# Second feed-forward of a decoder layer: 19 gate/up tiles as seven products of halves

## The chip, the cores and the metric

One core of a Trainium2 chip runs the whole layer in one launch. The metric is the device time of one execution in microseconds, lower is better. Everything is float32; the matmuls take float32r operands.

## The reference, cut to what matters

```python
for l in range(DEPTH):
    ...
    y = rmsnorm(h, ffn1_pre_g[l]) * (1.0 + sc1) + sh1
    y = swiglu(y, ffn1_w_gate[l], ffn1_w_up[l], ffn1_w_down[l])
    h = h + FFN_RESIDUAL_WEIGHT * g1 * rmsnorm(y, ffn1_post_g[l])
    ...
    y = rmsnorm(h, ffn2_pre_g[l]) * (1.0 + sc3) + sh3
    y = swiglu(y, ffn2_w_gate[l], ffn2_w_up[l], ffn2_w_down[l])
    h = h + FFN_RESIDUAL_WEIGHT * g3 * rmsnorm(y, ffn2_post_g[l])

def swiglu(y, w_gate, w_up, w_down):
    return (jax.nn.silu(y @ w_gate) * (y @ w_up)) @ w_down
```

512 tokens, width 1024, hidden width 2816. Between the two feed-forwards stands a token mixing by mLSTM and HGRN2 heads. The shift, scale and gate vectors come from a product of the conditioning c with `ada_w`.

## The kernel before, in words

Each float32 product is made of three matmuls (`mm3`, L110 to L113): an operand is split into a rounded part hi (a cast to float32r) and a rest lo (raw minus hi), and hi x hi, hi x lo and lo x hi are added up in PSUM. `unit` (L95) loads 128 x 1024 weights into one of four raw buffers (pool `wraw`) by SyncE's DMA queue, casts them to hi on ScalarE (L106) and subtracts to lo on VectorE (L107); hi and lo have four buffers each in the pool `wsp`.

The activations stay in SBUF transposed, width on the partitions: `y` is a pair of tiles of 8 k-tiles x 512 tokens. `y_token_tile` (L189) makes them for 128 tokens: TensorE transposes, scale and shift out of PSUM (four k-tiles on ScalarE, four on VectorE), rounding and rest.

The second feed-forward (`ffn2`, L798) has 22 tiles of 128 hidden units, each with a gate and an up part. Its first three tiles (`FF2_F`) run in two halves of 256 tokens, since tokens 256 to 511 come late: two `y_token_tile` calls are still in `later` and are issued between their matmuls. Four of their six weight units lie in `wsp`; those of the third tile lie in parts of `hT` that are not yet used. The other 19 tiles go through `up_tile` (L227): two units, two PSUM tiles, 2 x 8 x 3 matmuls of 512 columns, then `swiglu_evac` (L216): sigmoid on ScalarE, two products on VectorE, a cast on ScalarE and a subtract on VectorE, into the pair `hT`. After each of the first 11 of these tiles one step of `rest` is issued: eight `ada` (L118, a 512 KB load and four multiply-reduces on VectorE), `gate_rows`, nothing, and `gate_load`.

`down` (L236) multiplies `hT` with the down weights: two halves of 512 output columns, 11 units of two hidden tiles each, four token tiles of 128, in four PSUM tiles; the last four units run token tile by token tile, so that the normalisation (`post`, L284) of one goes beside the next.

The order on each engine is that of a list scheduler, which places instructions by their place in the program where nothing holds them back. A buffer is handed on when the last reader in the program is done. PSUM has six `mm` buffers and two `tr` buffers. `phase` reserves some bytes ahead of a pool, so that the tiles behind it lie at other addresses.

Of the kernel before, what the change touches and what calls it, by code (L numbers as in the profile page):

```python
# [7 lines left out]
F32 = mybir.dt.float32  # L8
F32R = mybir.dt.float32r
# [5 lines left out]
P = 128  # L15
# [6 lines left out]
NH = 4  # L22
EPS = 1e-6
START_F = 3
GAP_W = 160
GAP_Y = 64
GAP_H = 128
GAP_M = 64
FF2_F = 3

# [2 lines left out]
def layer_kernel(ctx: ExitStack, tc: tile.TileContext, x, c, cols, gate_b,  # L33
# [14 lines left out]
    def phase(pool, name, nbytes):  # L48

        if nbytes:  # L50
            pool.tile([P, nbytes // 4], F32, name=name)

    phase(gap, "gap_w", GAP_W)

# [55 lines left out]
    def mm3(ps, lhs, rhs, start, stop):  # L110
        nc.tensor.matmul(ps, lhs[0], rhs[0], start=start, stop=False)  # L111
        nc.tensor.matmul(ps, lhs[0], rhs[1], start=False, stop=False)  # L112
        nc.tensor.matmul(ps, lhs[1], rhs[0], start=False, stop=stop)  # L113
# [42 lines left out]
    def rstd_of(ss, n, w, name):  # L156
# [32 lines left out]
    def y_token_tile(s, i, y, n):  # L189

        ts_ = slice(i * P, (i + 1) * P)
        for q in range(2):
# [19 lines left out]
            nc.vector.tensor_tensor(out=y[1][:, q * 4:q * 4 + 4, ts_], in0=yf, in1=hv.bitcast(F32),  # L212
                                    op=ALU.subtract)


    def swiglu_evac(f, psg, psu, hT, tag):  # L216
# [16 lines left out]
                    k == 0, k == KT - 1)  # L233
        swiglu_evac(f, ps[0], ps[1], hT, tag)

    def down(wd, hT, tag, s, nxt, n=NF, order=lambda f: f, pump=None, drain=None, rest=()):  # L236


        t0, ss0, later = [], [], []
# [1 line left out]
        for half in range(2):  # L241
            acc = [mm_tile(f"pd{tag}_{half}_{i}") for i in range(NT)]

            def step(u, i, v):
                for e in range(2):
                    f = order(2 * u + e)
                    mm3(acc[i], (hT[0][:, f, i * P:(i + 1) * P], hT[1][:, f, i * P:(i + 1) * P]),
                        (v[0][:, e, :], v[1][:, e, :]), u == 0 and e == 0, u == nu - 1 and e == 1)

            last = []  # L250
            for u in range(nu):
                v = unit(wd[half, u], 1024, f"d{tag}_{half}_{u}")
                v = tuple(a.rearrange("p (e n) -> p e n", e=2) for a in v)
                if rest:
                    rest.pop(0)()
                if u < nu - 4 or (drain and half == 0):
                    if drain and u == nu - 1:
                        drain()
                    for i in range(NT):
                        step(u, i, v)  # L260
                        if pump:
                            pump()
                else:
                    last.append((u, v))
            for i in range(NT):
# [530 lines left out]


    def ffn2(y, later):  # L798
        with tc.tile_pool(name="hT2", bufs=1) as hp:
            phase(hp, "gap_h2", GAP_H)  # L800
            hT = (hp.tile([P, NF, T], F32R, name="hThi2"), hp.tile([P, NF, T], F32R, name="hTlo2"))
            us = []
            for f in range(FF2_F):
                us.append([])
                for g in range(2):
                    dst = None
                    if f == FF2_F - 1:
                        sl = slice(NF - 2 * (g + 1), NF - 2 * g)
                        dst = tuple(a[:, sl, :].rearrange("p a b -> p (a b)") for a in hT)
                    us[f].append(k3(unit(wgu2[f, g], 1024, f"b_{f}_{g}", dst)))  # L810
# [15 lines left out]
            for f in range(FF2_F, NF):  # L826
                up_tile(f, wgu2, y, hT, "b")
                if rest:
                    rest.pop(0)()
            down(wd2, hT, "b", 2, None)  # L830

    ffn2(*mix(*ffn1()))

# [74 lines left out]
```

## Time and profile before

| | us |
|---|---|
| median of 3 runs | 1054.83 (1054.58 to 1054.88) |
| the profiled execution | 1054.96 |
| its span, first to last instruction | 1053.2 |
| 19 tiles, first matmul to the down projection's first | 717.3 to 926.0 |
| down projection | 926.0 to 1046.9 |

Times in rows count from the span's start. PE is TensorE's matmul, PEld its weight load, DVE VectorE, ACT ScalarE, POOL GpSimd, SP SyncE. L111 is line 111 of the kernel. A row of a timeline has start, duration, engine, line, operation, what is written and read, shapes, and in brackets the idle time before it and what ended it. Matmuls are pipelined: their starts are closer together than they last.

### The profile page before, as it was taken

What the parts mean: (1) busy time and instruction counts of PE and PEld (TensorE: products, weight loads), DVE (VectorE), ACT (ScalarE), POOL (GpSimd) and SP (SyncE); (2) the same over time, 40 slices, a digit from 0 to 9 for tenths busy, and PEclk for the clock granted to TensorE, in tenths of its full rate; (3) what the DMA queues carried; (4) which work ended last, traced back from release to release, by engine and by line L of the source; (5) the groups of instructions that cost most, each with busy time, mean ns of one, the idle gap of its engine ahead of it and who ended that gap; (6) DMA issues with size and microseconds to landing.
All of it is one profiled execution on the core that took longest, in us unless ns stands there. A gap on an engine that the chain in (4) does not pass through costs nothing.

```text
span 1053.2 us, 13118 instructions
## 1 busy us (share of the span) xinstructions
PE 1031.8 (98%) x4988; PEld 857.2 (81%) x4988; DVE 600.4 (57%) x1426; ACT 344.8 (33%) x496; POOL 70.7 (7%) x104
## 2 busy tenths in 40 slices
PE   6999999999999999999999999999999999999997
PEld 4778888888888878978888887898888888888886
DVE  7975465566555285387879775775543433332323
ACT  5542233222212164435343223632322222221311
POOL 1000000000000020022223131100000000000000
PEclk9999999999999999999999999999999999999999
DMA  9864445555655413333223311144454223322212
GB/s 343 279 212 152 147 153 156 164 158 165 197 180 166 149 63 126 107 124 111 100 81 100 101 61 61 44 153 146 138 111 149 92 89 101 100 99 81 100 40 80
DMA packets 42938, 136.39 MB, mean 130 GB/s; under 512 B 7670, under 2 KB 8054, under 8 KB 42876
## 3 DMA queue, kind: packets, MB, share of 16 engines
q1 hardware_dynamic: 42588, 135.41, 39.7%
q8 instruction: 39, 0.64, 0.2%
q10 hardware_dynamic: 288, 0.16, 0.1%
q14 instruction: 23, 0.19, 0.1%
HBM read 133.43 MB, written 2.12 MB: 129 GB/s over the span
## 4 chain that ended last, share of the span: by engine, by line
PE 86%; DVE 8%; issue 1%; DMA 1%; POOL 1%; ACT 1%; DVEq 0%; POOLq 0%; SPq 0%; ACTq 0%
PE pub L111 7%; PE pub L113 7%; PE pub L112 7%; PE pua L112 7%; PE pua L111 7%; PE pua L113 7%; PE pft L113 4%; PE pft L112 4%; PE pft L111 4%; PE pdb L112 4%; PE pdb L111 4%; PE pdb L113 4%; PE pda L111 4%; PE pda L113 3%; PE pda L112 3%; PE pl L576 3%
## 5 line engine op out<-in xcount | busy, mean ns | idle before, releaser
L111 PE MATMUL pub<-yhi,h_b 128*128 128x512 f32 (+1 forms) x368 | 137.8, 375 | 0.0
L113 PE MATMUL pub<-yhi,l_b 128*128 128x512 f32 (+1 forms) x368 | 137.0, 372 | 0.0
L112 PE MATMUL pub<-ylo,h_b 128*128 128x512 f32 (+1 forms) x368 | 136.0, 370 | 0.0
L111 PE MATMUL pua<-yhi,h_a 128*128 128x512 f32 x304 | 119.3, 392 | 0.7 <-DVE ta L219 0.7
L112 PE MATMUL pua<-ylo,h_a 128*128 128x512 f32 x304 | 119.8, 394 | 0.0
L113 PE MATMUL pua<-yhi,l_a 128*128 128x512 f32 x304 | 118.0, 388 | 0.0
L106 ACT CAST h_b<-r_b 128x1024 fp32r<-128x1024 f32 x42 | 44.0, 1051 | 137.8 <-issue 102.3
L107 DVE TENSOR_TENSOR l_b<-r_b,h_b 128x1024 fp32r<-128x1024 f32 x42 | 51.3, 1224 | 60.3 <-ACT h_b L106 60.3
L132 DVE CUSTOM_DVE_ANT_0 a<-a,sc 128x256 f32<-128x256 f32 x216 | 82.4, 425 | 0.0
L113 PEld LDWEIGHTS pub<-yhi,l_b 128*128 128x128 f32 x368 | 69.1, 188 | 13.4
L111 PE MATMUL pft<-yhi,h_ft 128*128 128x512 f32 x192 | 79.6, 415 | 0.0
L112 PEld LDWEIGHTS pub<-ylo,h_b 128*128 128x128 f32 x368 | 69.1, 188 | 13.0 <-DVE ylo L212 0.2
L106 ACT CAST h_a<-r_a 128x1024 fp32r<-128x1024 f32 x38 | 39.9, 1049 | 119.5 <-issue 74.9
L111 PEld LDWEIGHTS pub<-yhi,h_b 128*128 128x128 f32 x368 | 69.1, 188 | 11.3
L113 PE MATMUL pft<-yhi,l_ft 128*128 128x512 f32 x192 | 76.3, 397 | 0.0
L112 PE MATMUL pft<-ylo,h_ft 128*128 128x512 f32 x192 | 75.8, 395 | 0.0
L111 PE MATMUL pda<-h_da,hThi 128*128 128x512 f32 x176 | 69.5, 395 | 0.0
L112 PE MATMUL pdb<-l_db,hThi 128*128 128x512 f32 x176 | 69.3, 394 | 0.0
L113 PE MATMUL pda<-h_da,hTlo 128*128 128x512 f32 x176 | 69.0, 392 | 0.0
L111 PE MATMUL pdb<-h_db,hThi 128*128 128x512 f32 x176 | 69.0, 392 | 0.0
L111 PEld LDWEIGHTS pua<-yhi,h_a 128*128 128x128 f32 x304 | 57.1, 188 | 14.5 <-DVE ta L219 1.2
L112 PE MATMUL pda<-l_da,hThi 128*128 128x512 f32 x176 | 68.3, 388 | 0.0
(270 smaller groups left out, 1946.5 us busy)
## 6 DMA issues: line engine op xcount, KB each, us to landing
a<-in_ada_w_dram SPq DMA_DIRECT2D x70, 512.0 KB, 3.8
r_b<-in_wgu_dram SPq DMA_DIRECT2D x44, 512.0 KB, 3.5
r_a<-in_wgu_dram SPq DMA_DIRECT2D x38, 512.0 KB, 4.1
r_ft<-in_w_ft_dram SPq DMA_DIRECT2D x24, 512.0 KB, 3.8
r_da<-in_wd_dram SPq DMA_DIRECT2D x22, 512.0 KB, 3.4
r_db<-in_wd_dram SPq DMA_DIRECT2D x22, 512.0 KB, 3.5
r_dm<-in_w_out_dram SPq DMA_DIRECT2D x8, 512.0 KB, 4.4
r_s<-in_wgu_dram SPq DMA_DIRECT2D x12, 256.0 KB, 6.1
```

Source lines behind the costliest of these rows:

```text
L106: nc.scalar.copy(hi, raw)
L107: nc.vector.tensor_tensor(out=lo, in0=raw, in1=hi.bitcast(F32), op=ALU.subtract)
L111: nc.tensor.matmul(ps, lhs[0], rhs[0], start=start, stop=False)
L112: nc.tensor.matmul(ps, lhs[0], rhs[1], start=False, stop=False)
L113: nc.tensor.matmul(ps, lhs[1], rhs[0], start=False, stop=stop)
L132: nc.vector.tensor_tensor_reduce(out=raw[:, sl], in0=raw[:, sl], in1=sc[:, sl], scale=1.0, scalar=init if q == 0 else 0.0, op0=ALU.mult, o ...
L576: nc.tensor.matmul(pv[:, i, :], kk[:, sl], qq[:, sl], start=True, stop=True)
```

## The change

The 19 tiles are computed by Winograd's form of Strassen's scheme: seven products of halves in place of eight. A tile's weights are four blocks of 512 x 128: B11 and B21 are the upper and lower half (in k) of the gate weights, B12 and B22 those of the up weights; the activations are split into A11, A12 (first 256 tokens, k-tiles 0 to 3 and 4 to 7), A21 and A22. Sums of the A blocks (S1 to S4) are made once, sums of the B blocks (T1 to T4) for every tile, each split into hi and lo. A product is 4 k-tiles x 3 matmuls of 256 columns. The results are added up partly in PSUM and partly on ScalarE and VectorE. `hT` becomes one float32 tile, split into hi and lo per down unit and half (`split`). The ada and gate steps go into `down`.

```diff
-GAP_W = 160
+GAP_S = 160
+GAP_W = 32
+GAP_X = 192
...
+    phase(small, "gap_s", GAP_S)
...
-    def down(wd, hT, tag, s, nxt, n=NF, order=lambda f: f, pump=None, drain=None, rest=()):
+    def down(wd, hT, tag, s, nxt, n=NF, order=lambda f: f, pump=None, drain=None, rest=(), split=None):
...
+                    if split:
+                        x = tuple(a[:, e, i * P:(i + 1) * P] for a in v[2])
...
+                if split:
+                    v = (*v, split(half, u))
+                for _ in range(2 if split and u < 3 else 1):
+                    if rest:
+                        rest.pop(0)()
...
     def ffn2(y, later):
...
+            def sums(i, yfs):
...
+                tt(out=r[:, 0], in0=yfs[0], in1=yfs[1], op=ALU.add)
+                tt(out=r3, in0=hi1, in1=yfs[0], op=ALU.subtract)
+
+                def rest_of():
+                    tt(out=r[:, 1], in0=r[:, 0], in1=hi1, op=ALU.subtract)
+                    nc.scalar.copy(Shi[:, 0, :, a], r[:, 0])
+                    tt(out=r[:, 1], in0=r[:, 1], in1=lo1, op=ALU.subtract)
+                    tt(out=r3, in0=r3, in1=lo1, op=ALU.add)
+                    nc.scalar.copy(Shi[:, 1, :, a], r[:, 1])
+                    nc.scalar.copy(Shi[:, 2, :, a], r3)
...
+                    tt(out=s4[:, :, a], in0=hi2, in1=r[:, 1], op=ALU.subtract)
+                    tt(out=s4[:, :, a], in0=s4[:, :, a], in1=lo2, op=ALU.add)
+
+                late.append(rest_of)
...
+            us = [[k3(unit(wgu2[f, g], 1024, f"b_{f}_{g}")) for g in range(2)] for f in range(FF2_F)]
...
-                                later.pop(0)()
+                                later.pop(0)(hook=sums)
...
-                        swiglu_evac(f, ps[f][0], ps[f][1], hT, "b")
+                        t = small.tile([P, T], F32, tag="x2", name=f"sg_{f}")
+                        nc.scalar.activation(t, ps[f][0], AF.Silu)
+                        tt(out=hT[:, f, :], in0=t, in1=ps[f][1], op=ALU.mult)
+                if hf == 0:
+                    for fn in late:
+                        fn()
...
+                def load(self):
+                    pool, tag = ((hp, "Rb"), (small, "G"))[(self.f - FF2_F) % 2]
+                    self.Rb = pool.tile([P, D], F32, tag=tag, name=f"Rb{self.f}", bufs=1)
+                    nc.sync.dma_start(self.Rb, wgu2[self.f, 1])
...
+                def split(self, hl, raw):
+                    for sl in (slice(0, T), slice(T, 2 * T)):
+                        nc.scalar.copy(hl[0][:, sl], raw[:, sl])
+                    tt(out=hl[1], in0=raw, in1=hl[0].bitcast(F32), op=ALU.subtract)
+
+                def prep1(self):
+                    self.split(self.pair("B11", "B21", wsp, ("hi", "lo"), "1"), self.Ra)
+                    h4, l4 = self.pair("B22", None, small, ("ysb", "ysb"), "4", bufs=4)
+                    nc.scalar.copy(h4, self.Rb[:, T:])
...
+                def prep2(self):
...
+                    tt(out=Rb[:, T:], in0=Rb[:, T:], in1=Rb[:, :T], op=ALU.subtract)
+                    tt(out=Rb[:, :T], in0=Rb[:, :T], in1=Ra[:, :T], op=ALU.subtract)
+                    tt(out=Ra[:, :T], in0=Rb[:, T:], in1=Ra[:, :T], op=ALU.add)
+                    tt(out=Ra[:, T:], in0=Ra[:, T:], in1=Ra[:, :T], op=ALU.subtract)
+
+                def prep3(self):
+                    self.split(self.pair("T2", "T4", hp, ("X3h", "X3l"), "3", bufs=2), self.Ra)
+
+                def prep4(self):
+                    self.split(self.pair("T1", "T3", wsp, ("hi", "lo"), "2"), self.Rb)
+
+                def prep5(self):
+                    h4, l4 = self.b22
+                    nc.scalar.activation(l4, h4.bitcast(F32), AF.Copy, scale=-1.0)
+                    nc.gpsimd.dma_start(l4, wgu2[self.f, 1, :, T:], accum_op=ALU.add)
...
+                def p6(self):
+                    product(self.A[:, :HT], self.w["T2"], ya["S2"], False)
+                    nc.scalar.copy(self.s[:, 1], self.A[:, :HT])
...
+                def p7(self):
+                    product(self.A[:, :HT], self.w["T3"], ya["S3"], False)
...
+                    nc.scalar.copy(s3, self.A[:, :HT])
+                    tt(out=self.g[:, 3], in0=self.B[:, :HT], in1=s3, op=ALU.add)
+
+                def p4(self):
+                    product(self.A[:, :HT], self.w["T4"], ya["A22"], False)
+                    nc.scalar.activation(self.g[:, 2], self.A[:, :HT], AF.Silu)
+                    nc.scalar.activation(self.g[:, 0], self.g[:, 0], AF.Silu)
+
+                def p3(self):
+                    product(self.B[:, :HT], self.w["B22"], ya["S4"], False)
+                    tt(out=self.g[:, 1], in0=self.B[:, :HT], in1=self.s[:, 1], op=ALU.add)
...
+            for f in range(FF2_F, NF - 1):
+                w, v = W.pop(0), W[0]
+                w.p6()
+                if f + 2 < NF:
+                    W[1].load()
+                if f + 3 < NF:
+                    W.append(Tile(f + 3))
+                v.prep1()
+                w.p5()
+                v.prep2()
+                w.p7()
+                v.prep3()
+                v.open()
+                v.p1()
+                v.p2()
+                v.prep4()
+                w.p4()
+                v.prep5()
+                w.p3()
...
+            todo = [w.p4, w.p3]
...
+            def split(half, u):
+                c = (half * (NF // 2) + u + 3) % 5
...
+                src = hT[:, 2 * u:2 * u + 2, :]
+                nc.scalar.copy(hi, src)
+                tt(out=lo, in0=src, in1=hi.bitcast(F32), op=ALU.subtract)
+                return hi, lo
...
-            for f in range(FF2_F, NF):
-                up_tile(f, wgu2, y, hT, "b")
-                if rest:
-                    rest.pop(0)()
-            down(wd2, hT, "b", 2, None)
+            down(wd2, None, "b", 2, None, rest=rest, split=split, pump=pump)
```

`tt` is VectorE's tensor_tensor; `product` is the loop over 4 k-tiles of `mm3`; P1 and P2 (B11 x A11, B21 x A12) open a tile's two PSUM tiles A and B, and P5 is T1 x S1 into B. `Ra` and `Rb` are the raw gate and up weights, six buffers in all (`Ra` four in `wraw`, `Rb` one of its own and one of the gate rows' buffer G).

## Rows read from the trace of the kernel before

**Rows 1.** Engine totals of the page: busy us, share of the span, instructions.
```profile
PE 1031.8 (98%) x4988; PEld 857.2 (81%) x4988; DVE 600.4 (57%) x1426; ACT 344.8 (33%) x496; POOL 70.7 (7%) x104
```
**Rows 2.** By stretch: length, busy PE, PEld, DVE, ACT, POOL, clock, DMA share, GB/s.
```profile
676.00:718.00 42.00, 41.21 (x326) 39.54 (x326) 32.66 (x68) 20.88 (x36) 3.34 (x3) 1.00 0.46 150
718.00:926.00 208.00, 208.00 (x910) 170.70 (x909) 90.39 (x149) 58.78 (x75) 0.00 (x0) 1.00 0.37 112
926.00:1047.00 121.00, 121.00 (x529) 98.98 (x528) 33.92 (x37) 25.14 (x34) 1.65 (x3) 1.00 0.23 79
```
**Rows 3.** Instructions of tile pub from 717.2 us: count, ns min/median/max, first and last start.
```profile
L111 PE MATMUL pub<-yhi,h_b x304: 394/394/397, 717.3 to 925.4; 128*128 128x512 f32 x152
L113 PE MATMUL pub<-yhi,l_b x304: 392/392/392, 717.8 to 925.8; 128*128 128x512 f32 x152
```
**Rows 4.** TensorE's timeline, matmuls of 256 columns: 58 and 48 starts, first and last.
```profile
704.76 0.28 PE L113 MATMUL pub<-yhi,l_b 128*128 128x256 f32 x1
...
711.47 0.28 PE L113 MATMUL pub<-yhi,l_b 128*128 128x256 f32 x1
711.59 0.28 PE L111 MATMUL pub<-yhi,hThi 128*128 128x256 f32 x1
...
717.17 0.28 PE L113 MATMUL pub<-yhi,hTlo 128*128 128x256 f32 x1
```
**Rows 5.** VectorE's timeline in the 19 tiles.
```profile
800.80 1.23 DVE L107 TENSOR_TENSOR l_b<-r_b,h_b 128x1024 fp32r<-128x1024 f32 x1 [3.66 <-ACT h_b L106]
801.94 0.68 DVE L219 TENSOR_TENSOR tb<-tb,pub 128x512 f32<-128x512 f32 x1
...
806.30 1.23 DVE L107 TENSOR_TENSOR l_b<-r_b,h_b 128x1024 fp32r<-128x1024 f32 x1 [0.21 <-ACT h_b L106]
```
**Rows 6.** Groups by form from 676 to 1053 us, operations out of PSUM.
```profile
L218 ACT ACTIVATE tb<-pub 128x512 f32<-128x512 f32 x22 | 13.0, 591 | 1.1 <-PE pub L113 1.1
L203 ACT ACTIVATE yf<-pst,modc 128x128 f32<-128x128 f32 x12 | 4.8, 450 | 3.8 <-PE pst L197 3.8
L206 DVE TENSOR_SCALAR yf<-pst,modc 128x128 f32<-128x128 f32 x12 | 4.3, 403 | 0.0
```
**Rows 7.** ScalarE's timeline in the 19 tiles, casts of 1024 and 512.
```profile
805.21 1.05 ACT L106 CAST h_b<-r_b 128x1024 fp32r<-128x1024 f32 x1 [3.95 <-issue]
806.17 0.61 ACT L221 CAST hThi<-tb 128x512 fp32r<-128x512 f32 x1
```
**Rows 8.** DMA issues of the whole span: KB each, median us from issue to landing.
```profile
r_b<-in_wgu_dram SPq DMA_DIRECT2D x44, 512.0 KB, 3.5
r_s<-in_wgu_dram SPq DMA_DIRECT2D x12, 256.0 KB, 6.1
gd<-modc SPq DMA_DIRECT2D x3, 4.0 KB, 12.1
```
**Rows 9.** TensorE's timeline: the third tile's first matmul.
```profile
694.58 0.29 PE L111 MATMUL pub<-yhi,hThi 128*128 128x256 f32 x1
```
**Rows 10.** VectorE's timeline while the last token tile is made.
```profile
694.00 0.48 DVE L132 CUSTOM_DVE_ANT_0 a<-a,sc,col 128x256 f32<-128x256 f32 x1 [0.56 <-DMA a<-in_ada_w_dram]
...
695.71 0.42 DVE L209 CAST yhi<-yf 128x512 fp32r<-128x512 f32 x1
...
696.37 0.68 DVE L212 TENSOR_TENSOR ylo<-yf,yhi 128x512 fp32r<-128x512 f32 x1
...
698.70 0.69 DVE L212 TENSOR_TENSOR ylo<-yf,yhi 128x512 fp32r<-128x512 f32 x1 [0.15 <-ACT yhi L211]
```
**Rows 11.** Busy time by stretch around 450 us (columns as in rows 2).
```profile
450.00:452.00 2.00, 0.61 (x5) 0.18 (x4) 2.00 (x6) 1.84 (x3) 0.00 (x0) 1.00 0.00 1
452.00:454.00 2.00, 2.00 (x11) 1.68 (x12) 2.00 (x6) 0.00 (x0) 0.00 (x0) 0.68 0.04 11
454.00:456.00 2.00, 2.00 (x6) 1.59 (x5) 0.48 (x3) 0.18 (x1) 0.00 (x0) 0.50 0.82 246
```

More of the change, by code (lines that the diff above doesn't have):

```diff
@@ L50, in phase @@
         if nbytes:
-            pool.tile([P, nbytes // 4], F32, name=name)
+            pool.tile([P, nbytes // 4], F32, name=name, bufs=1)
     phase(gap, "gap_w", GAP_W)
@@ L108, in unit, with mm3 @@
         return hi, lo
[L110 to L113, printed above, removed]
+    def mm3(ps, lhs, rhs, start, stop, **kw):
+        nc.tensor.matmul(ps, lhs[0], rhs[0], start=start, stop=False, **kw)
+        nc.tensor.matmul(ps, lhs[0], rhs[1], start=False, stop=False, **kw)
+        nc.tensor.matmul(ps, lhs[1], rhs[0], start=False, stop=stop, **kw)
     modc = [const.tile([P, 3, KT], F32, name=f"modc{s}") for s in range(3)]
@@ L187, in y_tiles, with y_token_tile @@
                 ypool.tile([P, KT, T], F32R, tag="ylo", name=f"ylo{s}"))
[L189 removed]
+    def y_token_tile(s, i, y, n, hook=None):
         ts_ = slice(i * P, (i + 1) * P)
+        yfs = []
         for q in range(2):
@@ L213, in y_token_tile @@
                                     op=ALU.subtract)
+            yfs.append(yf)
+        if hook is not None:
+            hook(i, yfs)
     def swiglu_evac(f, psg, psu, hT, tag):
@@ L798, in ffn2, with s_tile, quarter, sum4 @@
     def ffn2(y, later):
+        HT = T // 2
+        K2 = KT // 2
         with tc.tile_pool(name="hT2", bufs=1) as hp:
[L800 to L810, printed above, removed]
+            tt = nc.vector.tensor_tensor
+            def s_tile(tag, at):
+                t = hp.tile([P, 3136], F32R, tag=tag, name=f"{tag}{at}")
+                return t[:, at:at + 3072]
+            Shi, Slo = (s_tile(t, 0).rearrange("p (a k t) -> p a k t", a=3, k=K2) for t in ("Shi", "Slo"))
+            hT = hp.tile([P, NF, T], F32, name="hT2")
+            phase(hp, "gap_x", GAP_X)
+            s4 = tmp_tile("s4").rearrange("p (k t) -> p k t", k=K2)
+            def quarter(a, th, kh):
+                return a[:, kh * K2:(kh + 1) * K2, th * HT:(th + 1) * HT]
+            late = []
+            def sums(i, yfs):
+                a = slice((i - 2) * P, (i - 1) * P)
+                hi1, lo1 = (v[:, 0:K2, a].bitcast(F32) for v in y)
+                hi2, lo2 = (v[:, K2:, a].bitcast(F32) for v in y)
+                r = hp.tile([P, 2, K2, P], F32, tag="X3h", name=f"sr{i}", bufs=2)
+                r3 = hp.tile([P, K2, P], F32, tag="X3l", name=f"sq{i}", bufs=2)
+                tt(out=r[:, 0], in0=yfs[0], in1=yfs[1], op=ALU.add)
[7 more added lines that the diff above has]
+                    nc.scalar.copy(Shi[:, 2, :, a], r3)
+                    tt(out=Slo[:, 0, :, a], in0=r[:, 0], in1=Shi[:, 0, :, a].bitcast(F32), op=ALU.subtract)
+                    tt(out=Slo[:, 1, :, a], in0=r[:, 1], in1=Shi[:, 1, :, a].bitcast(F32), op=ALU.subtract)
+                    tt(out=Slo[:, 2, :, a], in0=r3, in1=Shi[:, 2, :, a].bitcast(F32), op=ALU.subtract)
+                    tt(out=s4[:, :, a], in0=hi2, in1=r[:, 1], op=ALU.subtract)
+                    tt(out=s4[:, :, a], in0=s4[:, :, a], in1=lo2, op=ALU.add)
+                late.append(rest_of)
+            def sum4():
+                nc.scalar.copy(quarter(y[0], 1, 0), s4)
+                tt(out=quarter(y[1], 1, 0), in0=s4, in1=quarter(y[0], 1, 0).bitcast(F32), op=ALU.subtract)
+            us = [[k3(unit(wgu2[f, g], 1024, f"b_{f}_{g}")) for g in range(2)] for f in range(FF2_F)]
@@ new lines, in ffn2, with product @@
+            ya = {"A11": tuple(quarter(a, 0, 0) for a in y), "A12": tuple(quarter(a, 0, 1) for a in y),
+                  "S4": tuple(quarter(a, 1, 0) for a in y), "A22": tuple(quarter(a, 1, 1) for a in y)}
+            for n_, nm in enumerate(("S1", "S2", "S3")):
+                ya[nm] = (Shi[:, n_], Slo[:, n_])
+            def product(ps, w, x, start):
+                for k in range(K2):
+                    c = slice(k * P, (k + 1) * P)
+                    mm3(ps, (w[0][:, c], w[1][:, c]), (x[0][:, k, :], x[1][:, k, :]), start and k == 0, k == K2 - 1,
+                        skip_group_check=True)
@@ new lines, in ffn2 @@
+            W = [Tile(f) for f in range(FF2_F, FF2_F + 3)]
+            w, v = W[:2]
+            for fn in (w.load, v.load, w.prep1, w.prep2, sum4, w.prep3, w.prep4, w.prep5):
+                fn()
+            w.open()
+            w.p1()
+            w.p2()
+            for f in range(FF2_F, NF - 1):
[17 more added lines that the diff above has]
+                w.p3()
@@ new lines, in ffn2, with pump @@
+            w = W[0]
+            w.p6()
+            w.p5()
+            w.p7()
+            todo = [w.p4, w.p3]
+            def pump():
+                if todo:
+                    todo.pop(0)()
+            hd = [s_tile(t, 32).rearrange("p (c a b) -> p c a b", c=3, a=2) for t in ("Shi", "Slo")]
+            def split(half, u):
+                c = (half * (NF // 2) + u + 3) % 5
+                if c < 3:
+                    hi, lo = hd[0][:, c], hd[1][:, c]
+                else:
+                    hi, lo = (hp.tile([P, 1024], F32R, tag=t, name=f"hs{t}{half}_{u}", bufs=2)
+                              .rearrange("p (a b) -> p a b", a=2) for t in ("X3h", "X3l"))
+                src = hT[:, 2 * u:2 * u + 2, :]
+                nc.scalar.copy(hi, src)
+                tt(out=lo, in0=src, in1=hi.bitcast(F32), op=ALU.subtract)
+                return hi, lo
```

41 lines of the change are left out of this document (35 added, 6 removed).

## The prediction

> **What bounds the kernel now.** I read the engine totals of the page first [rows 1]: TensorE is busy for 98% of the span, VectorE for 57%, ScalarE for 33%. A busy TensorE could still hide waits inside, so the table by stretches comes next [rows 2]: from 718 to 926 us, where the 19 tiles lie that the change rewrites, TensorE has no idle time at the full clock, VectorE works 43% and ScalarE 28% of it; the down projection from 926 to 1047 looks the same. So matmul issue ends last in both, and what counts is the time from one matmul's start to the next. In the 19 tiles: the first starts at 717.3 us, the last of 912 at 925.8, which is 208.5 / 911 = 0.2289 us for a matmul of 512 columns [rows 3], 48 x 0.2289 = 10.99 us a tile. What 256 columns cost can be read from the three tiles before them, which run in two column halves: 58 starts from 704.76 to 711.47 give 0.1177 us; with the weights that lie in hT, 48 starts from 711.59 to 717.17 give 0.1187 [rows 4]. Two halves thus cost 3% more than one whole.
>
> **The change, part by part.** The sum is made against the profiled execution: 1054.96 us with a span of 1053.2, 0.13 over the median of 1054.83.
>
> **Seven products.** A tile had 2 x 8 x 3 = 48 matmuls of 512 columns; it gets 7 products x 4 k-tiles x 3 = 84 of 256. 84 x 0.1177 = 9.89 us against 10.99 is -1.10 us, for 19 tiles -20.9 us. With 0.1187 it is 9.97 and -19.4. The saving is an eighth in columns, a tenth in time. The Trainium skill ("TensorE: Matmul & The Clock Gate", section Back-to-back issue gap) gives columns / 2.4 GHz + 2.5 ns for one start to the next. By that rule a tile goes from 10.36 to 9.17 us and the 19 would save 22.5 us; the trace has 0.2289 and 0.1177 us where the rule gives 0.2158 and 0.1092, so the rows decide.
>
> **VectorE in the loop.** A tile had two 1024-wide remainders and three 512-wide operations. Now it has three of 1024 (rests of B11/B21, T2/T4, T1/T3), four sums of 512, the 512 product, and three adds of 256 from PSUM: eleven. A 1024-wide subtract takes 1.23 us and the next starts 1.14 after it; a 512 takes 0.68 [rows 5]. A 256 from PSUM has no row: 128 wide takes 0.40 [rows 6], 512 wide 0.68; I take 0.45, as the fixed part shows in the 128. Sum 3 x 1.23 + 5 x 0.68 + 3 x 0.45 = 8.4 us, less 0.09 of overlap for each of eleven: 7.5 us of 9.89. The three adds at 0.68 would make it 8.2. It fits beside TensorE, with 0.22 us to spare per instruction; a wait of VectorE for ScalarE's cast shows as 0.21 us [rows 5].
>
> **ScalarE in the loop.** Two casts of 1024, one sigmoid and one cast become eight passes of 512 (0.61 us [rows 7]), three copies of 256 from PSUM and two Silus of 256 (0.45 at 128 wide, 0.59 at 512 [rows 6, 7]; I take 0.5). Together 7.4 us, with the overlap near 6.2 of 9.89. The tight place is the bank A: p6 ends, ScalarE copies it to s, and p7 may only then write on; between them TensorE has p5, 12 x 0.1177 = 1.41 us, of which 0.16 goes until p6's last result is out (a 256 matmul lasts 0.28 [rows 4]). The copy has 1.25 us: 0.5 for itself and at most one 0.61 pass ahead of it. Its cover is that one pass; were a whole 1024 cast (1.05 [rows 7]) ahead of it, p7 would wait 0.3 us.
>
> **The rest by accumulating DMA.** POOL issues one a tile, 256 KB, with nothing else in its queue; behind it waits only the last product p3 of that tile. It stands behind p4 of the tile before, ScalarE's two Silus and its own negation (1.6 us together), and p3 comes seven products later, 9.9 us: 8.3 us to land in. No accumulating DMA is in the trace. 256 KB loads take 6.1 us in the crowded first stage, 512 KB ones 3.5 here; the slowest group of issues of any kind has a median of 12.1 [rows 8]. Cost from 0 to 12.1 - 8.3 = 3.8 us a tile; nearest to it are the loads from the same weights, so 0. It can't gain anything, as nothing that TensorE did goes away with it. SP issues two loads of 512 KB a tile as before, now one and two tiles ahead; the 11 ada and gate steps, with nine of its loads, go to the down projection.
>
> **The first three tiles.** Six split buffers were four plus two in hT; now there are four in all. The third tile's two units can't be split before the first tile's second half has been multiplied, so TensorE has the 96 products of tiles 1 and 2 and then needs the last tokens. In the trace the third tile starts at 694.58 [rows 9] and hides this: the upper half of token tile 3 is rounded at 695.71, its rest is out at 696.37 + 0.68 = 697.05, the lower half at 698.70 + 0.69 = 699.39 [rows 10]. Without the ada passes that VectorE does between them (from 694.00), but with two new adds per token tile in their place, I put the upper half's rest at 696.0 and expect TensorE to go on with k 0 to 3 of four units, 48 x 0.1177 = 5.6 us, while the lower half comes. Stall 696.0 - 694.6 = 1.4 us; bounds 0 (if the scheduler finds other work) and 699.4 - 694.6 = 4.8. After an idle of 1.4 us at 450 us the granted clock fell to 0.50, that is 1.2 GHz, and stood there up to 456 [rows 11], some eight matmuls of 512 at 0.43 us in place of 0.23: 1.6 us. Half of that goes in: +2.2 us.
>
> **The first seven-product tile.** VectorE has from about 698.6 to the first p6: sixteen 512-wide operations for the sums of two token tiles (16 x 0.60), two hook adds, two unit rests, two gate products, three tile rests, four sums and S4's rest: 9.6 + 1.2 + 2.3 + 1.2 + 3.4 + 2.4 + 1.1 = 21.2 us, so 719.8. The tile opens at 717.3 + 1.4 = 718.7 and its p6 comes 2.83 later, at 721.5. That leaves 1.7 us for VectorE's waits for ScalarE, which are short of what I expect: +1.0, bounds 0 and 4.
>
> **The down projection** keeps its 528 matmuls at the same width. VectorE gains a second 1024-wide rest per unit, 2 x 1.23 = 2.5 us of 24 x 0.229 = 5.5, ScalarE a second cast of 1.05; the ada steps add near 2 us in eight units, at most 4 in the first three, where 6.5 us of VectorE stand against 5.5 of TensorE; the last tile, which prepares no successor, lets it run ahead by more than that 3 us. Cost 0; without this cover 3. The loop's handoffs beyond these I put at +1.0 for all 18 of them, from 0 to 5 (0.3 each, the p7 wait above). The new gaps move addresses; what that does to the matmul's start distance has its size in the 0.1187 against 0.1177.
>
> **Sum.** -20.9 + 2.2 + 1.0 + 1.0 = -16.7; 1054.96 - 16.7 = 1038.3 us.
>
> **The rivals.** *VectorE and the handoffs set the pace.* Eleven operations in order, most behind ScalarE or TensorE: at 0.27 us of idle each a tile lasts 7.5 + 3.0 = 10.5 us, +0.6 x 19 = 11: 1049 (1043 to 1053 for 0.24 to 0.29). For it: two dependent chains cross every product. Against: in the 42 us before 718 VectorE was busy 78% with 68 operations [rows 2], as dense as here, while TensorE ran 98% of that time, and most of the next tile's work can be done a tile early. *The rest lands late.* TensorE stands before p3 in every tile. It decides from 8.3 us of landing, and the change turns into a loss from 8.3 + 16.7 / 19 = 9.2; at 10 us it is +1.7 x 19 = 32, so 1070. For it: nothing in the trace shows how fast a DMA is that reads, adds and writes. Against: half the bytes of loads that land in 3.5 us, on engines under 40% busy [rows 2, 8]. *The products gain nothing*: 84 products must then take 10.99 / 84 = 0.131 us each, because each brings a weight load for half the columns, or the relocated buffers slow them: 1055. Against: the 0.1177 was measured with exactly one load per 256 columns.
>
> **How the numbers follow.** Forecast 0.69, VectorE and handoffs 0.18, late rest 0.09, no gain 0.04. The forecast's own range is 1033.5 (all overheads at 0) to 1042 (0.1187, and a longer first stall). The range 1033.5 to 1047 adds most of the first rival and leaves out its upper end and the other two, 0.19. A difference of 0.2%, 2.1 us, is about what a measurement of this kernel can tell from none. Faster by more: 0.69 + 0.18 = 0.87; within: 0.04; slower: 0.09.
>
> **What would show it.** Right: from the first seven-product tile to the down projection about 188 us in place of 208.8, starts 0.118 us apart, TensorE idle near 0 and VectorE near 76%; one gap of 1 to 2 us near 695. Wrong: TensorE waiting before p3 for the DMA, before p7 for ScalarE's copy, or before p6 for a rest from VectorE in every tile; a granted clock under 1.00 after 720 us; matmuls of the down projection further apart than 0.229.

## The result, and the profile after

The changed kernel takes 1035.93 us in the median of four runs (1035.53 to 1037.47) against 1054.70 (1054.11 to 1054.88): a ratio of 0.9826, with a 95% interval from 0.9809 to 0.9843. The forecast was 1038.3 us and the range 1033.5 to 1047. The profiled execution took 1035.53 us with a span of 1033.8.

The engine totals of the changed kernel answer to [rows 1]:

```profile
PE 1011.2 (98%) x5672; PEld 873.7 (85%) x5672; DVE 699.1 (68%) x1577; ACT 431.0 (42%) x694; POOL 86.6 (8%) x123
```

TensorE's share is the same 98%, VectorE went from 57 to 68 and ScalarE from 33 to 42. The table by stretches has the columns of [rows 2]; its three stretches are those from the first three tiles, from the first seven-product tile (717.4) and from the down projection's first matmul (902.7):

```profile
676.00:717.40 41.40, 39.68 (x320) 38.03 (x319) 40.03 (x67) 27.32 (x48) 4.53 (x5) 1.00 0.41 119
717.40:902.70 185.30, 185.24 (x1574) 185.04 (x1573) 148.31 (x229) 116.90 (x236) 14.80 (x17) 1.00 0.49 136
902.70:1027.00 124.30, 123.39 (x554) 101.71 (x552) 66.02 (x110) 46.08 (x57) 1.66 (x3) 1.00 0.34 113
```

In the middle stretch TensorE is busy for all but 0.06 us, at the full clock, though VectorE now works 80% of it (148.3 of 185.3) and ScalarE 63%. The last tile's products p4 and p3 lie behind the first matmul of the down projection, 24 x 0.118 = 2.83 us. Put back where they belong, the stretches compare so (starts of the matmuls, us):

| stretch | before | after | difference | the sum had |
|---|---|---|---|---|
| first three tiles | 36.42 | 37.39 | +0.97 | +2.2 |
| 19 tiles | 208.75 | 185.32 + 2.83 = 188.15 | -20.60 | -20.9 + 1.0 + 1.0 |
| down projection, to the last matmul's start | 120.63 | 124.19 - 2.83 = 121.36 | +0.73 | 0 |
| together | 365.80 | 346.90 | -18.90 | -16.7 |

The other 0.5 of the 19.4 us between the two profiled executions is no part of the change: the first three tiles began at 680.00 in place of 680.88, and from the last matmul's start to the end it took 6.85 us in place of 6.50. Such offsets differ from run to run, and medians scatter by one or two us with them, so experiments a few us apart are read from these stretches.

**Where TensorE waits.** TensorE's timeline at the last token tile, and below it the row of that stretch in the table by stretches:

```profile
693.02 0.28 PE L115 MATMUL pub<-yhi,l_b 128*128 128x256 f32 x1
694.40 0.74 PE L113 MATMUL pub<-yhi,h_b 128*128 128x256 f32 x4 [1.11 <-DVE yhi L214]
695.32 0.39 PE L114 MATMUL pub<-ylo,h_b 128*128 128x256 f32 x1 [0.17 <-DVE ylo L217]
```

```profile
692.00:696.00 4.00, 2.72 (x21) 2.31 (x20) 4.00 (x10) 2.61 (x7) 0.00 (x0) 1.00 0.45 77
```

The gap of 1 to 2 us near 695 that the prediction named is there, and VectorE ends it. It did not cost its clock: the granted clock is 1.00 in the four microseconds around it, where an idle of 1.4 us at 450 us had been followed by 0.50 [rows 11].

Next, the first seven-product tile, in VectorE's and in TensorE's timeline:

```profile
720.09 1.21 DVE L911 TENSOR_TENSOR l<-Rb,h 128x1024 fp32r<-128x1024 f32 x1
721.22 0.41 DVE L950 TENSOR_TENSOR g<-pB,s 128x256 f32<-128x256 f32 x1
```

```profile
721.35 0.28 PE L115 MATMUL pA<-Shi,l 128*128 128x256 f32 x1
721.69 0.39 PE L113 MATMUL pB<-Shi,h 128*128 128x256 f32 x1
```

VectorE makes the rest of T1 until 721.30, and behind it the add that reads P2's result out of bank B (L950) is done at 721.63. p5, which writes into that bank, starts at 721.69, 0.34 after the matmul before it where 0.12 is usual. No wait in the other tiles of the loop is as long as that. The last wait is at the handoff to the down projection, in the timelines of TensorE, ScalarE and SyncE's queue:

```profile
903.85 0.40 PE L115 MATMUL pdb<-h_db,hsX3l 128*128 128x512 f32 x1
905.17 0.39 PE L113 MATMUL pA<-yhi,h 128*128 128x256 f32 x1 [0.92 <-ACT s L962]
```

```profile
900.08 0.37 ACT L954 COPY s<-pA 128x256 f32<-128x256 f32 x1 [1.08 <-PE pA L115]
903.80 1.05 ACT L108 CAST h_db<-r_db 128x1024 fp32r<-128x1024 f32 x1 [3.35 <-DMA r_db<-in_wd_dram]
904.75 0.36 ACT L962 COPY s<-pA 128x256 f32<-128x256 f32 x1
```

```profile
895.93 1.43 SPq L126 DMA_DIRECT2D a<-in_ada_w_dram  x2
898.05 0.33 SPq L102 DMA_DIRECT2D r_db<-in_wd_dram  x1
```

What that queue waited for between 880 and 908 us (total, times, longest), and the landing times of the down loads then:

```profile
SPq L102 <- DVE part L134: 3.4, 2, 2.8
DMA to landing us min/median/max: 3.5/4.4/5.7
```

p7 ended near 902.9, but ScalarE copies its result out of bank A at 904.75 only: in its queue the cast of a down unit stands ahead of the copy, and that cast waits 3.35 us for its load. The load was issued behind two ada loads; ada and down loads also share the four raw buffers of `wraw`, and the queue waited for VectorE's ada passes (L134) before it issued this load; and it took 5.7 us to land, the longest of that stretch. The last tile's p4 needs the bank and starts 1.1 us late. In the other tiles two products of the next tile lie between p7 and p4; here it is one group of six matmuls.

**The loop's operations.** Four groups by form from 717.4 to 902.7 (count | busy, mean ns | idle before and releaser):

```profile
L911 DVE TENSOR_TENSOR l<-Ra,h 128x1024 fp32r<-128x1024 f32 x36 | 43.6, 1215 | 0.0
L910 ACT CAST h<-Ra 128x512 fp32r<-128x512 f32 x70 | 40.1, 618 | 2.1 <-DVE Ra L924 0.9 <-DVE Ra L925 0.2
L950 DVE TENSOR_TENSOR g<-pB,s 128x256 f32<-128x256 f32 x19 | 7.9, 416 | 2.0 <-PE pB L115 2.0
L946 ACT COPY s<-pA 128x256 f32<-128x256 f32 x19 | 7.1, 372 | 1.3 <-PE pA L115 1.3
```

256 columns out of PSUM take VectorE 0.42 us and ScalarE 0.37, where the sum had 0.45 and 0.5. The accumulating DMA: ScalarE's timeline just behind the p3 of the first seven-product tile, POOL's timeline with the third and the tenth of its 19 issues, the landing times of the 17 issues in the loop, and a p3 in TensorE's timeline:

```profile
730.36 0.62 ACT L916 CAST h<-Rb 128x512 fp32r<-128x512 f32 x1 [0.91 <-PE pB L114]
```

```profile
731.95 0.86 POOL L936 DMA_DIRECT2D l<-in_wgu_dram  x1 [41.08 <-ACT l L935]
801.30 0.86 POOL L936 DMA_DIRECT2D l<-in_wgu_dram  x1 [9.02 <-ACT l L935]
```

```profile
DMA to landing us min/median/max: 3.9/4.0/5.3
```

```profile
817.90 0.28 PE L113 MATMUL pB<-yhi,h 128*128 128x256 f32 x1
```

The four buffers for B22's hi and rest hold two tiles. So the cast of B22 (L916) waits until a p3 has read its operands, and the negation and the DMA that follow are for the tile two further on. The first two seven-product tiles were served by two issues ahead of the loop, at 686.60 and 689.97; the third issue, at 731.95 behind the first tile's p3 (728.87), is the third tile's, and the tenth, at 801.30, is the tenth tile's, whose p3 starts at 817.90: 16.6 us after the issue. The longest landing took 5.3, so at least 11 us are to spare.

### The profile page after: what moved, and what is told of

Same layout as the page of the kernel before. It is cut to its first block, busy times and chain, and to the rows that moved or that the text cites. A ratio compares the mean times of both kernels' runs of the same rounds, so it can differ in the third digit from the quotient of the medians.

```text
span 1033.8 us, 14910 instructions
## 1 busy us (share of the span) xinstructions
PE 1011.2 (98%) x5672; PEld 873.7 (85%) x5672; DVE 699.1 (68%) x1577; ACT 431.0 (42%) x694; POOL 86.6 (8%) x123
## 4 chain that ended last, share of the span: by engine, by line
PE 84%; DVE 9%; DMA 2%; issue 2%; ACT 1%; POOL 1%; DVEq 0%; POOLq 0%; SPq 0%; ACTq 0%
PE pua L114 7%; PE pua L113 7%; PE pua L115 7%; PE pft L114 4%; PE pft L113 4%; PE pft L115 4%; PE pdb L114 4%; PE pdb L113 4%; PE pdb L115 4%; PE pda L113 4%; PE pda L115 4%; PE pda L114 3%; PE pA L115 3%; PE pA L113 3%; PE pA L114 3%; PE pl L590 3%
## 5 line engine op out<-in xcount | busy, mean ns | idle before, releaser
L113 PE MATMUL pua<-yhi,h_a 128*128 128x512 f32 x304 | 119.3, 392 | 0.0
L134 DVE CUSTOM_DVE_ANT_0 a<-a,sc 128x256 f32<-128x256 f32 x216 | 82.4, 423 | 0.0
L115 PEld LDWEIGHTS pua<-yhi,l_a 128*128 128x128 f32 x304 | 57.1, 188 | 12.8
L114 PEld LDWEIGHTS pua<-ylo,h_a 128*128 128x128 f32 x304 | 57.2, 188 | 11.3
L109 DVE TENSOR_TENSOR l_a<-r_a,h_a 128x1024 fp32r<-128x1024 f32 x38 | 46.4, 1222 | 24.1 <-ACT h_a L108 24.1
L108 ACT CAST h_da<-r_da 128x1024 fp32r<-128x1024 f32 x22 | 23.1, 1050 | 77.7 <-PE pda L115 58.5
L109 DVE TENSOR_TENSOR l_da<-r_da,h_da 128x1024 fp32r<-128x1024 f32 x22 | 26.9, 1224 | 33.2 <-ACT h_da L108 33.0
L911 DVE TENSOR_TENSOR l<-Ra,h 128x1024 fp32r<-128x1024 f32 x38 | 46.0, 1216 | 0.0
L910 ACT CAST h<-Ra 128x512 fp32r<-128x512 f32 x76 | 43.7, 618 | 3.6 <-PE pub L114 1.4
L134 DVE CUSTOM_DVE_ANT_0 a<-a,sc,col 128x256 f32<-128x256 f32 x48 | 23.2, 483 | 31.1 <-DMA a<-in_ada_w_dram 31.1
L113 PE MATMUL pA<-yhi,h 128*128 128x256 f32 x152 | 42.5, 280 | 0.9 <-ACT s L962 0.9
L115 PEld LDWEIGHTS pft<-yhi,l_ft 128*128 128x128 f32 x192 | 36.3, 189 | 8.3 <-DVE l_ft L109 0.2
```

The source lines that it names most:

```text
L108: nc.scalar.copy(hi, raw)
L115: nc.tensor.matmul(ps, lhs[1], rhs[0], start=False, stop=stop, **kw)
L134: nc.vector.tensor_tensor_reduce(out=raw[:, sl], in0=raw[:, sl], in1=sc[:, sl], scale=1.0, scalar=init if q == 0 else 0.0, op0=ALU.mult, o ...
L910: nc.scalar.copy(hl[0][:, sl], raw[:, sl])
L911: tt(out=hl[1], in0=raw, in1=hl[0].bitcast(F32), op=ALU.subtract)
```

## The experiments

Each changes the changed kernel unless it says otherwise. The stretches are those of the table above, without putting back the 2.83 us: changed kernel 37.39 | 185.32 | 124.19.

**Is it the number of products?** The old kernel, its 19 tiles run in two column halves as the first three are: 96 matmuls of 256 columns a tile.

```diff
-            for k in range(KT):
-                mm3(ps[g], (us[g][0][:, k, :], us[g][1][:, k, :]), (y[0][:, k, :], y[1][:, k, :]),
+            for sl in (slice(0, 256), slice(256, 512)) if tag == "b" else (slice(0, 512),):
+                for k in range(KT):
+                    mm3(ps[g][:, sl], (us[g][0][:, k, :], us[g][1][:, k, :]), (y[0][:, k, sl], y[1][:, k, sl]),
```

> The kernel before, with the 19 tiles' 48 matmuls of 512 columns as 96 of 256 (same work, no scheme). By the start distances 0.1177 and 0.2289 a tile goes from 10.99 to 11.30 us: 5.9 us more than before, 1060.6. If a weight load per 256 columns cost more in a long stretch than in the three tiles it was read from: over 1063. If narrowing were free: 1054.7.

Measured: 1060.36 us, ratio 1.0058 (1.0040 to 1.0076); the 19 tiles took 214.83 us (716.64 to 931.47) in place of 208.75. In the table by stretches, from 730 to 880 us, this kernel and below it the changed one:

```profile
730.00:880.00 150.00, 150.00 (x1275) 150.00 (x1275) 65.15 (x110) 41.07 (x53) 0.00 (x0) 1.00 0.37 116
```

```profile
730.00:880.00 150.00, 150.00 (x1276) 150.00 (x1275) 118.39 (x167) 97.66 (x197) 13.04 (x15) 1.00 0.49 132
```

The same 150 us hold 1275 and 1276 matmuls. Halving the columns loses 6.1 us, and the eighth of the matmuls left out then gives 26.7 (214.83 to 188.15): the two parts of the seven-product term.

**How near is VectorE?** The matmuls of p6 and p7 go, 24 of 84 a tile, and nothing else.

```diff
-                    product(self.A[:, :HT], self.w["T2"], ya["S2"], False)
-                    product(self.A[:, :HT], self.w["T3"], ya["S3"], False)
```

> The matmuls of p6 and p7 are left out; their operands are still made and their copies still run. TensorE then needs 60 x 0.1177 = 7.06 us a tile, VectorE 7.5. If the engines fit beside each other as the prediction counts them, VectorE becomes the bound near 7.5 to 8.3 us with its waits: 30 to 45 us less, 991 to 1006. If TensorE alone still set the pace: 2.83 x 19 = 54 less, 982. If VectorE and handoffs had been at the edge already: less than 20 us gained, 1016 or over.

Measured: 990.12 us over two runs, ratio 0.9392 (0.9372 to 0.9413); stretches 37.91 | 138.58 | 124.03. The table by stretches within the loop, which ends at 856.26 us here, and VectorE's timeline from one operation to the same one a tile later:

```profile
730.00:850.00 120.00, 117.59 (x969) 114.11 (x968) 119.33 (x174) 92.21 (x208) 13.74 (x17) 1.00 0.64 169
```

```profile
799.47 0.69 DVE L925 TENSOR_TENSOR Ra<-Ra 128x512 f32<-128x512 f32 x1
...
807.12 0.68 DVE L925 TENSOR_TENSOR Ra<-Ra 128x512 f32<-128x512 f32 x1
```

60 matmuls would be 7.1 us a tile, but the tile takes 7.65, and VectorE is busy for 119.3 of 120 us, TensorE for 117.6. VectorE becomes the bound about where its operations had been counted, 7.5 us. At 9.9 us a tile it has some 2.2 to spare, which is why the rival of VectorE and the handoffs did not come about.

**The accumulating DMA.** First without it: the rest of B22 as a subtract on VectorE.

```diff
                     nc.scalar.copy(h4, self.Rb[:, T:])
+                    tt(out=l4, in0=self.Rb[:, T:], in1=h4.bitcast(F32), op=ALU.subtract)
...
-                    nc.scalar.activation(l4, h4.bitcast(F32), AF.Copy, scale=-1.0)
-                    nc.gpsimd.dma_start(l4, wgu2[self.f, 1, :, T:], accum_op=ALU.add)
```

> The rest of B22 is a VectorE subtract of 512 in place of ScalarE's negation and the accumulating DMA. If TensorE's starts set the pace and VectorE only fits beside it: VectorE has 7.5 us of starts in a tile of 9.89, gets 0.6 more, still 1.8 us spare: 1035.9 within 1.5 us. If VectorE and its handoffs were at the edge (the first rival): 0.6 x 19 = 11 us more, 1047.

Measured: 1037.25 us (1032.42 to 1037.32), ratio 0.9829 (0.9808 to 0.9850); stretches 37.46 | 185.46 | 125.72. By stretches, 718 to 904 us, and ScalarE's timeline at the handoff:

```profile
718.00:904.00 186.00, 186.00 (x1576) 185.70 (x1575) 160.01 (x241) 104.27 (x220) 0.00 (x0) 1.00 0.34 107
```

```profile
905.96 1.04 ACT L108 CAST h_db<-r_db 128x1024 fp32r<-128x1024 f32 x1 [4.88 <-DMA r_db<-in_wd_dram]
```

VectorE is busy for 86% and TensorE still does not wait: the DMA is worth nothing in the loop as it stands. The 1.5 us more lie at the handoff, where the cast waits 4.88 us for its load and p4 starts 2.6 us late for the copy behind it.

Then late: the negation and the DMA only after p7 of the same tile (the negation takes a zero made from p7's copy as its bias, so that it cannot go ahead).

```diff
                 w.p4()
-                v.prep5()
                 w.p3()
...
                 w.p7()
+                w.prep5()
                 v.prep3()
```

> The negation that opens the accumulating DMA is held until the same tile's p7 has been copied out (its bias is a zero made from that copy), so the DMA has three products, 4.2 us, until p3. Negation 0.65, issue 0.87, landing 4.0 and the copy's own 0.6 make 6.1 us: if the second rival's mechanism is as priced, TensorE waits 1.5 to 2.5 us before p3 in every tile, 27 to 47 us more, 1063 to 1083. If the landing doesn't gate p3, 1036.

Measured: 1076.9 us, ratio 1.0218 (1.0201 to 1.0235); stretches 37.48 | 221.18 | 130.1. TensorE's timeline at two tiles' p3, and POOL's:

```profile
800.38 0.39 PE L115 MATMUL pB<-yhi,l 128*128 128x256 f32 x1 [1.57 <-DMA l<-in_wgu_dram]
...
811.94 0.39 PE L115 MATMUL pB<-yhi,l 128*128 128x256 f32 x1 [1.38 <-DMA l<-in_wgu_dram]
```

```profile
807.91 0.89 POOL L936 DMA_DIRECT2D l<-in_wgu_dram  x1 [10.93 <-PE pA L115]
819.47 0.89 POOL L936 DMA_DIRECT2D l<-in_wgu_dram  x1 [10.67 <-PE pA L115]
```

A tile lasts 11.56 us, and TensorE waits for the DMA in each of them: 1.26 to 1.65 us in 17 tiles, 4.55 and 3.78 in the last two, behind which the granted clock was near 0.50 for some microseconds. Without those two, 1.67 us a tile is still 32 for 19, more than the change gains. So the rival of the late rest is a real mechanism, and it would have ended slower than before; what kept it away is how early the DMA is issued, two tiles ahead.

**The short casts.** One cast of 1024 in place of two of 512.

```diff
-                    for sl in (slice(0, T), slice(T, 2 * T)):
-                        nc.scalar.copy(hl[0][:, sl], raw[:, sl])
+                    nc.scalar.copy(hl[0], raw)
```

> The casts of 1024 weights are one pass in place of two of 512. By the prediction's step on bank A, a 1.05 us cast ahead of p6's copy makes p7 wait up to 0.3 us a tile: between 0 and 5 us more, 1036 to 1041. If ScalarE's order leaves the copy free whatever the casts' length (it stood idle 0.25 us ahead of that copy in the changed kernel): 1035.9 within 1 us.

Measured: 1037.18 us, ratio 0.9844 (0.9829 to 0.9859); stretches 37.81 | 185.15 | 125.40: no wait in the loop, a longer one (2.3 us) at the handoff. ScalarE's timeline:

```profile
801.10 0.37 ACT L953 COPY s<-pA 128x256 f32<-128x256 f32 x1 [0.24 <-PE pA L115]
802.27 1.05 ACT L909 CAST h<-Rb 128x1024 fp32r<-128x1024 f32 x1 [0.80 <-DVE Rb L922]
803.23 1.04 ACT L909 CAST h<-Ra 128x1024 fp32r<-128x1024 f32 x1
804.17 0.36 ACT L961 COPY s<-pA 128x256 f32<-128x256 f32 x1
```

The copy that p7 waits for (801.10) has no cast ahead of it; the whole cast stands ahead of the next copy (804.17), whose bank is wanted only two products later.

**The ada steps.** Eight of them and the gate rows go back into the loop, one after each p3.

```diff
                 w.p3()
+                if rest:
+                    rest.pop(0)()
...
-            down(wd2, None, "b", 2, None, rest=rest, split=split, pump=pump)
+            down(wd2, None, "b", 2, None, rest=[lambda: gate_load(2)], split=split, pump=pump)
```

> The eight ada steps and gate_rows go back from the down projection to the tile loop, one a tile. VectorE gets about 1.6 us of starts in eight tiles: 9.1 of 9.89. If only TensorE's pace counts: 1035.9 to 1037. If VectorE with its waits for ScalarE can't be filled beyond some 85%: eight tiles of 10.4 or more, 1040 or over.

Measured: 1038.92 us (1036.98 to 1039.34), ratio 0.9853 (0.9838 to 0.9867); stretches 37.80 | 186.54 | 123.22. The loop has three waits of 0.2, 0.1 and 0.7 us and the handoff's is down to 0.1. VectorE's and TensorE's timelines at the longest:

```profile
794.70 0.48 DVE L134 CUSTOM_DVE_ANT_0 a<-a,sc,col 128x256 f32<-128x256 f32 x1 [1.55 <-DMA a<-in_ada_w_dram]
```

```profile
797.81 0.39 PE L113 MATMUL pA<-yhi,h 128*128 128x256 f32 x1 [0.58 <-ACT s L962]
```

VectorE, in its order, stands 1.55 us before an ada load; the sums behind it come late, with them the casts and ScalarE's copy, and p4 waits. In the loop the steps cost 1.2 us, and moved out they cost about 1.0 at the handoff. By the stretches there is almost nothing to gain between the two places. The median, 3.0 us above the changed kernel's, is not accounted for by them: the profiled run is the fastest of the four, and 1.2 us of it lie behind the last matmul (8.04 us to the end in place of 6.85).

**The two waits.** The third tile's weights in a part of `hT` again (eight of its rows as a tile of their own, which later hold hidden units):

```diff
-            hT = hp.tile([P, NF, T], F32, name="hT2")
+            ha = hp.tile([P, NF - 8, T], F32, name="hT2")
+            park = hp.tile([P, 8, T], F32R, tag="hT2b", name="park")
...
-            us = [[k3(unit(wgu2[f, g], 1024, f"b_{f}_{g}")) for g in range(2)] for f in range(FF2_F)]
+            us = [[k3(unit(wgu2[f, g], 1024, f"b_{f}_{g}", spare(f, g))) for g in range(2)] for f in range(FF2_F)]
```

> The split units of the third tile lie in the part of hT that is written last, as in the kernel before, so TensorE has that tile's first half while the last tokens come. If the gap near 695 us is the price of four split buffers: 1.3 to 1.8 us less, 1034.1 to 1034.6. If the time before the first seven-product tile is set by VectorE's sums instead: no change, 1035.9 within 0.7, and the wait moves to the first tile.

And p4 of the last tile one group of down matmuls later:

```diff
-            todo = [w.p4, w.p3]
+            todo = [lambda: None, w.p4, w.p3]
```

> In the down projection the last tile's p4 comes after two steps in place of one. If TensorE's 0.9 to 1.1 us wait at 904 us is p7's copy standing behind a cast that waits for its DMA: about 1 us less, 1034.9. If the step behind it then waits for the split of the second unit, whose buffer p4 holds: no change or up to 1 us more.

Measured: parked 1034.01 us, ratio 0.9804 (0.9783 to 0.9825), stretches 36.18 | 185.15 | 123.73; later 1035.20 us, ratio 0.9816 (0.9791 to 0.9840), stretches 37.96 | 185.15 | 123.01. TensorE's timeline with the third tile parked, and below it with p4 later:

```profile
692.14 0.28 PE L113 MATMUL pub<-yhi,h_b 128*128 128x256 f32 x1
692.88 0.65 PE L202 MATMUL pst<-ident,n 128*128 128x128 f32 x4 [0.46 <-DVE yf L211]
```

```profile
905.91 0.39 PE L115 MATMUL pdb<-h_db,hsX3l 128*128 128x512 f32 x1
906.14 0.28 PE L113 MATMUL pA<-yhi,h 128*128 128x256 f32 x1
```

Each takes away the wait it aims at, 1.2 us each in its stretch. (The first stretch alone, in the runs that leave it as it is, takes between 37.4 and 38.0 us.) Both together:

> Third tile's split units in hT and p4 one step later together: if both waits are what they seem, 2.3 to 2.8 us less than the changed kernel, 1033.1 to 1033.6; if one is only moved, 1034.5 to 1036.

Measured: 1033.62 us (1033.04 to 1036.47), ratio 0.9807 (0.9783 to 0.9831); stretches 36.13 | 185.15 | 123.02. Its profiled run, the one of 1036.47, began the first three tiles only at 683.54 us; its stretches are as short as in the two runs that take one wait away each.

**The reserves.** The three new reserves as they were before the change:

```diff
-GAP_S = 160
-GAP_W = 32
+GAP_S = 0
+GAP_W = 160
...
-GAP_X = 192
+GAP_X = 0
```

> The new reserves are taken back: no gap_s, gap_w 160 again, no gap_x. If addresses set the distance of matmul starts: those of the seven products or of the down projection move by up to 1% (0.1177 to 0.119, 0.229 to 0.233), up to 4 us more, 1036 to 1040. If not: 1035.9 within 1 us.

Measured: 1035.25 us (1034.62 to 1039.08), ratio 0.9825 (0.9798 to 0.9851); stretches 37.81 | 182.18 | 126.21. The time is the same, but the loop is 3.1 us shorter and the down projection 2.0 longer. So the reserves were taken apart, on top of the kernel with both waits gone: first S and W as in this diff with X at 192, then X alone at 0.

> Both waits are gone as in the run with the third tile parked and the fourth product late (stretches there 36.1 up to the first seven-product tile, 185.15 for the seven-product tiles, 123.0 for the down projection; median 1033.6). The two reserves ahead of the weights' buffers are set as in the run without the new gaps (together 32 bytes a partition less), the one ahead of the sums' buffers stays at 192. Theory A (the place of the weights' and activations' buffers sets the starts of the loop, the last reserve those of the down projection): loop 182.2, down 123.0, median 1030.6. Theory B (the first two reserves move both): loop 182.2, down 125.0, median 1032.7. Theory C (the last reserve does both): loop 185.15, down 123.0, median 1033.6.

> The other half of the same split: only the reserve ahead of the sums' buffers is taken out (192 to 0). Theory A: loop 185.15, down 125.0, median 1035.6. Theory B: nothing changes, loop 185.15, down 123.0, median 1033.6. Theory C: loop 182.2, down 125.0, median 1032.7.

Measured: S and W moved 1026.97 us (1026.62 to 1027.33), ratio 0.9742 (0.9728 to 0.9755), stretches 36.17 | 178.59 | 123.67; X moved 1031.76 us, ratio 0.9786 (0.9773 to 0.9800), stretches 36.14 | 181.39 | 125.25. The table by stretches, 150 us of the loop and 70 of the down projection; the changed kernel's loop row stands above, and its down projection's is the first here:

```profile
940.00:1010.00 70.00, 70.00 (x308) 57.66 (x308) 31.86 (x29) 26.95 (x33) 0.00 (x0) 1.00 0.23 79
```

No new reserves:

```profile
730.00:880.00 150.00, 150.00 (x1297) 150.00 (x1296) 120.61 (x174) 96.87 (x200) 13.91 (x16) 1.00 0.54 133
940.00:1010.00 70.00, 70.00 (x303) 56.68 (x302) 30.36 (x28) 25.38 (x31) 0.00 (x0) 1.00 0.21 68
```

X moved alone:

```profile
730.00:880.00 150.00, 150.00 (x1305) 150.00 (x1304) 122.24 (x177) 98.18 (x204) 14.10 (x16) 1.00 0.53 134
940.00:1010.00 70.00, 70.00 (x304) 56.77 (x303) 31.83 (x31) 25.57 (x33) 0.56 (x1) 1.00 0.20 63
```

S and W moved alone:

```profile
730.00:880.00 150.00, 150.00 (x1326) 150.00 (x1325) 124.56 (x179) 98.58 (x204) 14.10 (x16) 1.00 0.52 134
940.00:1010.00 70.00, 70.00 (x309) 57.64 (x308) 31.08 (x33) 24.75 (x33) 1.11 (x2) 1.00 0.21 68
```

TensorE is busy throughout in all of them; only how many matmuls fit differs. For the down projection theory A holds: with X at 192 there are 308 or 309 in 70 us, with X at 0 303 or 304. For the loop none of the three held: 1276 as in the changed kernel, 1305 with X moved, 1297 with all moved, 1326 with S and W moved. The counts take in matmuls that reach over an edge of the window; read from the starts between 730 and 850 us, the distances are 0.1178, 0.1152, 0.1159 and 0.1133 us. Each move alone shortens the loop, and the two together give less than either (the run with both is the one in which the waits were left in; the kernel with both waits gone has the changed kernel's 1276). The run with S and W moved is the fastest kernel of this study, 9 us below the changed one; of these, 6.6 are the loop (185.15 to 178.59 from the kernel with both waits gone). Which buffers must lie how to each other, and why, was not found.

## Why the prediction was right

The time lay in the range and 2.4 us below the forecast; the likeliest case was the one that came. The main term was right; the overheads were put at 4.2 us and came to 2.0, of which 0.7 in a place where the sum had nothing, so that part of the closeness is errors that cancel. (With all overheads at 0 the sum gives 1034.1, not the 1033.5 at which the range begins.)

- **Seven products**: right. Starts 0.1178 us apart against 0.1177, 20.6 us off the 19 tiles with their waits, against 20.9 without. From the first seven-product tile to the end of its last product it is 188.15 us where "about 188" was named. For 256 columns the Trainium skill ("TensorE: Matmul & The Clock Gate", Back-to-back issue gap), whose formula is given there for an isolated matmul, comes to an estimated 0.1092; no run here reached it, and the nearest is the 0.1133 of the moved reserves. That the distance came out so near the one read from three other tiles is in part luck: other reserves gave the same loop 0.1133 to 0.1178.
- **VectorE in the loop**: right. Counted 7.5 us a tile; with two products left out the tile takes 7.65 and VectorE is busy for 119.3 of 120 us. Its share was to be near 76% and is 79% (118.4 of 150 us).
- **ScalarE in the loop**: nearly right in size (97.7 of 150 us is 6.4 a tile, against 6.2), but the tight place was not the one named. The copy that p7 waits for has no cast ahead of it, and whole casts made no wait in the loop.
- **The rest by accumulating DMA**: right at a cost of 0, but not by the path that was priced. The prediction put it behind p4 of the tile before, with 8.3 us to land in. ScalarE's cast and negation wait for the p3 two tiles before instead and go ahead right behind it, which leaves 16.6 us from issue to p3. Landing took 4.0, at most 5.3. The late rest would thus have begun at twice the landing time that the rival named.
- **First three tiles**: right in its mechanism, too dear at 2.2 us. It cost 0.97; the clock's half share (0.8) did not come, and before had a short wait in the same place, which the sum did not take off. Parking the third tile gave the 1.2 us back.
- **First seven-product tile**: 0.3 us against 1.0. VectorE ends it, as forecast, but before p5 and with an add out of bank B behind T1's rest, not before p6 with a rest.
- **Handoffs of the loop**: put at 1.0, measured at nothing; the 18 tiles have room on both engines.
- **Down projection**: put at 0, measured at +0.73, and this is the step that failed. The cover named, VectorE's head start from the last tile, was there; the wait came from ScalarE, whose copy stood behind a cast that waited for a load. The nine loads that move there with the ada and gate steps were named in the prediction, but only their work on VectorE was priced, not that they take places in SP's queue and raw buffers ahead of the down weights; with the eight ada loads back in the loop the wait is 0.1 us. How much of it is the queue, the buffers or the slow landing was not separated. It is 1.1 us of +0.73; the rest, -0.4, are starts a little closer (227 ns in the groups that read the new buffers, against 229).
- **The gaps**: the sentence that their size is 0.1187 against 0.1177 fell short. In the loop alone, the reserves make between 0.1133 and 0.1178, some 7 us, and the change's own setting was the slowest of the four tried there.

The rivals: VectorE as the bound is 2.2 us a tile away; the late rest ends slower than before, as worked out, but came only when the issue was held until after p7; that the products gain nothing is refuted by the start distance.

## What to carry to other kernels

A stage in which one engine never waits can be priced by counting that engine's instructions and reading their start distance from a stretch of the same shape; then count the other engines against the new, shorter stage. The price that is easily missed lies at the stage's ends, where the next stage's loads and casts share a queue with the last handoffs. When TensorE is busy throughout and buffers have moved, count its matmuls in a fixed stretch: where the count changed here with the shapes, the clock and the busy share unchanged, only the reserves had moved, and a run for each reserve found 6.6 us.

## What the runs showed of the hardware that was not expected

- Reserves that move the SBUF buffers behind them by 32 to 224 bytes a partition change the start distance of float32r matmuls with a weight load each: 256 columns from 0.1133 to 0.1178 us (starts between 730 and 850 us), 512 columns from 0.2280 to 0.2323 (starts between 940 and 1010), and the same reserve can shorten one stage and lengthen another.
- An accumulating DMA of 256 KB on POOL's queue takes 0.86 us to issue and in the loop 4.0 us to land (3.9 to 5.3), half a microsecond more than 512 KB loads of the same weights (medians 3.5 and 3.6).
- An idle of 1.1 us on TensorE at 693 us left the granted clock at 1.00, where one of 1.4 us at 450 us had been followed by 0.50 [rows 11]. The length of the idle alone does not decide: with the late rest, 17 waits of 1.26 to 1.65 us, one in each tile, left the clock at 1.00 from 730 to 930 us.
